# A state-space scan whose output is kept feature-major: column-tiled y products, z as a feature projection, the norm applied by a broadcast row

## The chip, the core and the metric

The kernel runs on one core of a Trainium2 chip. The metric is the device time of one execution in microseconds (us). The names used for the engines are those of the profile: PE is TensorE (matmuls), PEld its weight loads, DVE is VectorE, ACT is ScalarE, POOL is GpSimd and SP is SyncE, which here only issues transfers.

## The reference, cut to what matters

One layer of a hybrid decoder over 2048 tokens and 16 meta tokens, width 1024. A normed input `u` goes through one wide projection. Its parts feed a Mamba-2 scan (SSD, 16 heads of 64 channels in 4 groups, state 128, chunks of 128), a gated linear attention (GLA, 4 heads), and gates; two branch projections are gated, summed and projected out. The part that the change touches is the SSD branch:

```python
seg = da_cum[..., :, None] - da_cum[..., None, :]
decay = exp(where(causal, seg, -inf))
scores = einsum('bzthn,bzshn->bhzts', cc, bc)
y_diag = einsum('bhzts,bzsh,bzshp->bzthp', scores * decay, dtc, xc)
y_off  = einsum('bzthn,bzhpn,bhzt->bzthp', cc, prev, exp(da_cum))
y = y_diag + y_off + d_skip[:, None] * xs
y = y * silu(z)
y_ssd = rmsnorm(y by groups of 256 channels) * ssd_norm_w
```

## The kernel before

The tokens are done in four blocks of 512 (block 0 with the 16 meta rows besides). In a block the projections stand in this order on TensorE: four SSD groups (`ssd_proj`, L456), then four GLA heads (`gla_proj`, L654). Projections are of two kinds. `proj_feat` (L192) keeps 128 x 128 weights stationary and moves 512 tokens, so its result has features on the partitions; a tile of 128 features takes 24 matmuls, since each product of two fp32 operands is made of three fp32r products (`accum`, L186 to L190). `proj_tok` (L204) keeps 128 tokens stationary and moves 256 columns of weights, so its result has tokens on the partitions; 256 columns take 96 matmuls. Before the change z (four times) and v (four times) come from `proj_tok`, and x, B, C, q, k and the gates from `proj_feat`. For group 0 the z columns come with the 32 columns of dt and of the low-rank gate (`zm`, L462).

The scans are generators. `step()` (L813) is called behind each piece of a projection and advances every running scan by one portion, so the scans' matmuls stand in between the projections'. The order of PE and SP is as written (a manual schedule); the order of the other engines' queues is set by a scheduler when the program is built, and every engine works its queue in order.

`ssd_scan` (L502) works on one group. `before(c)` transposes x and B of chunk c to token-major (L548), makes xdt, xw and the skip term (L551 to L554), and the masked decay `dm` (Relu L560, Exp L562, mask L563) from a row `cb` of decay sums that is copied from memory to all partitions (L500, issued from ScalarE's queue, three buffers). `after(c)` makes y with `dm` stationary and xdt moving (L572), the state's part with C stationary and the state moving (L573), and the state's update (L575, L577, L578). VectorE puts y together (L580 to L585), ScalarE sums its squares (L587). At the end comes the reciprocal root (`rstd_of`, L229 to L233, with the power on GpSimd), a scaling by token (L602), eight transposes to feature-major (L607) and a scaling by feature (L609), and the result is stored.

`gla_scan` (L663) has seven steps `level(1)` to `level(64)` (L709, matmul L712), one per portion, each in a chain with a masked copy (L720), a multiply (L725) and a packing (L706), and then products by chunk (L784 to L791) and transposes (L801). PSUM has eight banks in three pools: pj with three (projections), pt with three (transposes), pc with two (scores, y and state products, `level`, the GLA products).

After the blocks come gate, branch and output stages of 512-wide matmuls, which the change does not touch.

Of the kernel before, what the change touches and what calls it, by code (L numbers as in the profile page):

```python
# [26 lines left out]
NT4 = 5  # L27
NACT = 4
NC1 = 7
# [7 lines left out]
T_GATE = 32  # L37


@with_exitstack  # L40
def trunk_kernel(ctx: ExitStack, tc: tile.TileContext, xm, xmt, w_feat, w_tok, w_zm, w_br, w_o,
# [96 lines left out]
    pv = const.tile([P, 118], F32, name="pv")  # L138
# [6 lines left out]
    d_skip = pv[:, 102:118]  # L145
# [94 lines left out]
    def load_u(b):  # L240
# [34 lines left out]
        if m0:  # L275
            rs.append(rm_s)
            nc.sync.dma_start(cst[:, :2], cf32[:, :2])
            nc.sync.dma_start(pv, pvec)
            for q in range(NWR):
                raws[f"zm_{q}"] = load_raw(w_zm[:, q * 288:(q + 1) * 288])  # L280
# [72 lines left out]
    def new_block(b, u):  # L353
        o = Block()
        o.b, o.u = b, u
        o.m0 = META if b == 0 else 0
        o.tt = o.m0 + BLK
        o.segs_all = [(0, o.tt // 2), (o.tt // 2, o.tt // 2)] if b == 0 else [(0, BLK)]
        o.segs_real = [(o.m0, BLK)]
        o.starts = [o.m0 + c * P for c in range(NCH)]  # L360
        o.chunks = ([(0, META)] if o.m0 else []) + [(a, P) for a in o.starts]
        o.ci0 = 1 if o.m0 else 0
        o.nck = len(o.chunks)
        for nm in ("tkd", "tkc", "wde", "ecu", "dec"):
            setattr(o, nm, mk(bpool, [P, 5, NH], F32, nm, bufs=2))
        o.cumd = mk(dpool, [NH, BLK], F32, "cumd")
        o.g_all = mk(bpool, [P, GH, META + BLK], F32, "g_all")
        o.gla = {}
        o.alr = mk(bpool, [P, 5, 48], F32, "alr")
        o.mov = lambda kt, a, n: tuple(t[:, kt, a:a + n] for t in u)  # L370
        return o


    def dt_chain(o, psd):
        m0, nck, ci0 = o.m0, o.nck, o.ci0
        tkd, tkc, wde, ecu, dec = o.tkd, o.tkc, o.wde, o.ecu, o.dec
# [37 lines left out]
        nc.scalar.activation(ecu[:, :nck], tkc[:, :nck], AF.Exp)  # L414
# [6 lines left out]
        nc.scalar.dma_start(o.cumd, cr)  # L421

# [32 lines left out]

    def ssd_proj(o, g):  # L456
        m0, tt = o.m0, o.tt
        feats = []
        zs = mk(wk, [P, NCH, 256], F32, "tok4", bufs=NT4)
        if g == 0:  # L460
            pss = [bank(*pl) for pl in [(pj, "pj")] * 3 + [(pt, "pt")] + ([(pc, "pc")] if m0 else [])]
            yield from proj_tok("zm", w_zm, o.u, o.starts + [0] * o.ci0, list(enumerate(pss)), 288, 1, 256)  # L462
            begin(dt_chain(o, pss[NCH:] + pss[:NCH]))
            done = [(ps[:, :256], zs[:, c]) for c, ps in enumerate(pss[:NCH])]
        else:
            pss, places = halves_of(pj, "pj")
            yield from proj_tok(f"z{g}", w_tok[g], o.u, o.starts, places)
            done = [(ps, zs[:, 2 * r:2 * r + 2].rearrange("p c f -> p (c f)")) for r, ps in enumerate(pss)]
        for ps, dst in done:
            nc.scalar.activation(dst, ps, AF.Tanh, scale=0.5)  # L470
            nc.vector.scalar_tensor_tensor(dst, dst, 1.0, ps, op0=ALU.add, op1=ALU.mult)
        yield
        for j in range(4):
# [18 lines left out]
            feats.append(f)  # L492
            yield
        begin(ssd_scan(o, g, feats, zs))
# [3 lines left out]
    def fetch_cb(o, g, c):  # L498
        cbs[g, c] = cb = mk(wk, [P, 4, P], F32, "cb", bufs=3)
        nc.scalar.dma_start(cb, o.cumd[4 * g:4 * g + 4, c * P:(c + 1) * P].unsqueeze(0).to_broadcast([P, 4, P]))  # L500

    def ssd_scan(o, g, feats, zs):  # L502
        m0, ci0 = o.m0, o.ci0
        tkd, tkc, wde, ecu, dec = o.tkd, o.tkc, o.wde, o.ecu, o.dec
        x0, x1, bf, cf = feats
        fetch_cb(o, g, 0)
        yield
# [28 lines left out]
        yt = mk(wk, [P, NCH, 256], F32, "tok4", bufs=NT4)  # L536
        ssq = mk(sm, [P, 4], F32, "ssq")
        held = {}

        def before(c):  # L540
# [6 lines left out]
            for j, f in enumerate((x0, x1, bf)):  # L547
# [6 lines left out]
            nc.vector.tensor_tensor(yt[:, c].rearrange("p (h c) -> p h c", c=64), px,  # L554
                                    hb(d_skip[:, hs], P), op=ALU.mult)
# [10 lines left out]
        def after(c):  # L566
# [4 lines left out]
            for h in range(4):  # L571
                nc.tensor.matmul(py[:, h * 64:(h + 1) * 64], dm[:, h], xdt[:, h], start=True, stop=True)  # L572
            nc.tensor.matmul(py[:, 256:512], cf[:, a:a + P], s_ssd[:, g], start=True, stop=True)  # L573
# [5 lines left out]
            yo = mk(wk, [P, 4, 64], F32, "c1", bufs=NC1)  # L579
            nc.vector.tensor_tensor(yo, py[:, 256:512].rearrange("p (h c) -> p h c", c=64),  # L580
                                    hb(ecu[:, ci, hs], P), op=ALU.mult)
            yof = yo.rearrange("p a c -> p (a c)")
            nc.vector.tensor_tensor(yof, yof, py[:, 0:256], op=ALU.add)
            nc.vector.tensor_tensor(yof, yof, yt[:, c], op=ALU.add)
            nc.vector.tensor_tensor(yt[:, c], yof, zs[:, c], op=ALU.mult)  # L585
            jk = mk(wk, [P, 256], BF16, "junk", bufs=1)
            nc.scalar.activation(jk, yt[:, c], AF.Square, accum_out=ssq[:, c:c + 1])  # L587
# [12 lines left out]
        r = rstd_of(ssq, 4, 1.0 / 1024)  # L600
        for c in range(NCH):
            nc.scalar.activation(yt[:, c], yt[:, c], AF.Identity, scale=r[:, c:c + 1])  # L602
        yield
        for j in range(2):
            ps = bank(pt, "pt")
            for c in range(NCH):
                nc.tensor.transpose(ps[:, c * P:(c + 1) * P], yt[:, c, j * P:(j + 1) * P], ident)  # L607
            yo = mk(wk, [P, BLK], F32, "gg", bufs=4)
            nc.scalar.activation(yo, ps, AF.Identity, scale=hsw[:, 2 * g + j:2 * g + j + 1])  # L609
            nc.scalar.dma_start(y_left[0][o.b][2 * g + j], yo)  # L610


    def gla_keys(o, h):
# [8 lines left out]
        o.gla[h] = [], []  # L622
# [3 lines left out]
    def gla_values(o, h):  # L626
# [9 lines left out]
        yield from proj_tok(f"v{h}", w_tok[SG + h], o.u, o.starts + [0] * o.ci0, places)  # L636
# [17 lines left out]
    def gla_proj(o, h):  # L654
        ahead = o.b == nblk - 1 and h >= GH - 2
        if not ahead or h == GH - 2:
            yield from gla_keys(o, h)
        yield from gla_values(o, h)
        if ahead and h == GH - 2:
            yield from gla_keys(o, GH - 1)  # L660
        yield from gla_out_gates(o, h)

    def gla_scan(o, h, kq, vals, gs):  # L663
# [45 lines left out]
        def level(half):  # L709
            ps = bank(pc, "pc")  # L710
# [423 lines left out]
def _layout(inputs):  # L1134
# [23 lines left out]
    feat += [cols(o_m, 2048)]  # L1158
    w_zm = tiles(np.concatenate([cols(o_z, 256), cols(o_dt, 16), cols(o_a, 16)], axis=1), 288)[0]
    w_feat = tiles(np.concatenate(feat, axis=1), P)  # L1160
    w_tok = tiles(np.concatenate([cols(o_z, 1024), cols(o_v, 1024)], axis=1), 256)
# [27 lines left out]
    d_skip = np.broadcast_to(np.asarray(inputs["d_skip"])[0][None], (P, NH))  # L1189
# [6 lines left out]
    return {"xm": xm, "xmt": xmt, "w_feat": w_feat, "w_tok": w_tok, "w_zm": w_zm, "w_br": w_br, "w_o": w_o, "cf32": cf32, "cmsk": cmsk.reshape(P, -1),  # L1196
# [21 lines left out]
```

## Time and profile before

| | |
|---|---|
| median of 3 runs | 2353.59 us (2347.39 to 2354.49) |
| the profiled execution's own time | 2356.76 us |
| its span, first to last instruction | 2355.0 us |
| mean granted TensorE clock | 0.986 |
| share of the span busy: PE, DVE, ACT, POOL | 96%, 62%, 49%, 29% |

A row of the profile that groups instructions gives the line, engine, operation, what is written and read, shape and count, then busy time, mean duration in ns, and the idle time ahead of them with what ended it. In the waits a row gives who waited for whom, the total in us, how often, and the longest. In the windows a row gives the stretch, its length, busy time and count for PE, PEld, DVE, ACT and POOL, then the granted clock, the share of the DMA engines and GB/s. In the timeline a row gives start, duration, engine, line, operation and count. Matmuls are pipelined, so that the duration of one reaches over the start of the next.

### The profile page before, as it was taken

The page shows a single profiled execution, that of the slowest core. Times are in us where ns is not written, and L with a number is a line of the kernel's source. Part 1 is how long each engine was busy: PE and PEld are TensorE (multiplying, and loading weights), DVE is VectorE, ACT ScalarE, POOL GpSimd, SP SyncE. Part 2 cuts the span into 40 slices and gives each one's busy share as a digit, 9 for nine tenths or more (in the row PEclk, how much of TensorE's full clock was granted, in tenths as well). Part 3 has the DMA queues.
Part 4 walks back from the last instruction along what each step waited for, and adds up shares of the span by engine and source line. Part 5 has one row for each costly group of instructions (what it writes and reads, how often), then busy time and mean ns, then how long its engine had stood idle before and what let it go on. Part 6 is the DMA issues. An engine that isn't in the chain of part 4 may idle for free. (4 is left out here: it accounts for less than half of the span.)

```text
span 2355.0 us, 35946 instructions
## 1 busy us (share of the span) xinstructions
PE 2261.0 (96%) x12673; PEld 1963.7 (83%) x12673; DVE 1450.1 (62%) x2547; ACT 1143.9 (49%) x2582; POOL 678.5 (29%) x681
## 2 busy tenths in 40 slices
PE   7999999999899999999999999979999999999998
PEld 6889888898788988888888888868888888888876
DVE  5666655466554466655447654455578964779776
ACT  5656544365533265633346443354545454554443
POOL 4344333122211122221112200027433355323331
PEclk9999999999999999999999999989999999999999
DMA  8666765668676676766577644457677876688743
GB/s 305 228 207 225 254 226 200 215 206 252 213 242 201 210 223 216 255 213 222 173 226 245 209 143 165 134 168 249 209 246 264 292 235 214 225 284 272 257 155 123
DMA packets 301540, 518.01 MB, mean 220 GB/s; under 512 B 27696, under 2 KB 143664, under 8 KB 301360
## 3 DMA queue, kind: packets, MB, share of 16 engines
q1 hardware_dynamic: 200400, 402.84, 52.6%
q10 hardware_dynamic: 100960, 112.88, 13.8%
q8 instruction: 99, 1.62, 0.3%
q14 instruction: 81, 0.66, 0.1%
HBM read 368.42 MB, written 147.19 MB: 219 GB/s over the span
## 5 line engine op out<-in xcount | busy, mean ns | idle before, releaser
L188 PE MATMUL pj<-u,whl 128*128 128x512 f32 (+1 forms) x1184 | 448.7, 379 | 14.4 <-ACT acc L481 7.7
L190 PE MATMUL pj<-u,whl 128*128 128x512 f32 (+1 forms) x1184 | 432.9, 366 | 1.4 <-DVE dw L391 0.8
L189 PE MATMUL pj<-u,whl 128*128 128x512 f32 (+1 forms) x1184 | 432.2, 365 | 0.0
L188 PE MATMUL pj<-whl,u 128*128 128x256 f32 (+1 forms) x992 | 291.5, 294 | 2.2 <-ACT u L306 1.5
L190 PE MATMUL pj<-whl,u 128*128 128x256 f32 (+1 forms) x992 | 283.9, 286 | 1.4 <-DVE u L308 1.4
L189 PE MATMUL pj<-whl,u 128*128 128x256 f32 (+1 forms) x992 | 283.8, 286 | 0.9 <-POOL whl L169 0.9
L188 PEld LDWEIGHTS pj<-u,whl 128*128 128x128 f32 x1184 | 226.8, 192 | 52.1 <-ACT acc L481 9.3
L188 PE MATMUL pj<-b,a 128*128 128x512 f32 x640 | 252.9, 395 | 6.0 <-ACT sn L930 3.6
L190 PEld LDWEIGHTS pj<-u,whl 128*128 128x128 f32 x1184 | 226.2, 191 | 37.6 <-POOL whl L169 1.8
L189 PEld LDWEIGHTS pj<-u,whl 128*128 128x128 f32 x1184 | 226.7, 191 | 32.2
L189 PE MATMUL pj<-b,a 128*128 128x512 f32 x640 | 250.7, 392 | 1.8 <-DVE b L889 1.8
L190 PE MATMUL pj<-b,a 128*128 128x512 f32 x640 | 251.8, 393 | 0.0
L188 PEld LDWEIGHTS pj<-whl,u 128*128 128x128 f32 x992 | 191.6, 193 | 3.8 <-ACT u L306 2.0
L190 PEld LDWEIGHTS pj<-whl,u 128*128 128x128 f32 x992 | 191.2, 193 | 2.1 <-DVE u L308 2.1
L189 PEld LDWEIGHTS pj<-whl,u 128*128 128x128 f32 x992 | 191.6, 193 | 1.5 <-POOL whl L169 1.1
L80 POOL TENSOR_TENSOR wr<-wr 128x256 f32<-128x256 f32 x80 | 65.8, 823 | 433.7 <-DMA wr<-y 146.9
L169 POOL TENSOR_TENSOR whl<-wr,whl 128x512 fp32r<-128x512 f32 (+1 forms) x100 | 132.0, 1326 | 192.8 <-ACT whl L168 167.6
L889 DVE TENSOR_TENSOR b<-br,b 128x512 fp32r<-128x512 f32 x196 | 153.8, 805 | 45.9 <-ACT b L888 41.9
L904 POOL TENSOR_TENSOR as<-ar,ar 128x512 f32<-128x512 f32 x40 | 59.2, 1481 | 403.9 <-DMA ar<-in_w_br 151.7
L485 DVE SCALAR_TENSOR_TENSOR acc<-cin,hcw,acc 128x512 f32<-128x512 f32 (+1 forms) x192 | 155.7, 811 | 31.4 <-ACT acc L481 29.8
L888 ACT ACTIVATE b<-br 128x512 fp32r<-128x512 f32 x196 | 119.5, 626 | 99.9 <-DMA br<-br_t 36.4
L914 DVE TENSOR_TENSOR a<-ar,a 128x512 fp32r<-128x512 f32 x160 | 128.6, 812 | 59.2 <-ACT a L913 58.5
(270 smaller groups left out, 4903.5 us busy)
## 6 DMA issues: line engine op xcount, KB each, us to landing
whl<-k_s SPq DMA_DIRECT2D x96, 512.0 KB, 4.6
whl<-k_g SPq DMA_DIRECT2D x96, 512.0 KB, 4.0
whl<-k_v SPq DMA_DIRECT2D x48, 512.0 KB, 3.6
whl<-k_z SPq DMA_DIRECT2D x36, 512.0 KB, 3.8
wr<-in_w_feat SPq DMA_DIRECT2D x64, 256.0 KB, 4.3
k_s<-whl SPq DMA_DIRECT2D x32, 512.0 KB, 3.7
cb<-cumd ACTq DMA_DIRECT2D x64, 256.0 KB, 6.0
y<-gg ACTq DMA_DIRECT2D x64, 256.0 KB, 5.0
```

What stands on the lines that cost most here:

```text
L80: nc.gpsimd.tensor_tensor(o, x, y, op=ALU.subtract)
L169: nc.gpsimd.tensor_tensor(hl[:, 1], raw, hl[:, 0].bitcast(F32), op=ALU.subtract)
L188: nc.tensor.matmul(ps, sh, mh, start=first, stop=False, **kw)
L189: nc.tensor.matmul(ps, sh, ml, start=False, stop=False, **kw)
L190: nc.tensor.matmul(ps, sl, mh, start=False, stop=last, **kw)
L485: nc.vector.scalar_tensor_tensor(acc, cin[:, k:k + tt], hcw[:, ti, k:k + 1], acc, op0=ALU.mult, op1=ALU.add)
L888: nc.scalar.activation(t[:, 0], raw, AF.Copy)
L889: nc.vector.tensor_tensor(t[:, 1], raw, t[:, 0].bitcast(F32), op=ALU.subtract)
L904: nc.gpsimd.tensor_tensor(s1, a21, a22, op=ALU.add)
L914: nc.vector.tensor_tensor(t[:, 1], src, t[:, 0].bitcast(F32), op=ALU.subtract)
```

## The change

z becomes a feature projection: eight tiles of 128 features in each block through `proj_feat`, two behind the x, B and C tiles of each group. The place of z's group 0 beside the dt and low-rank columns is taken by v of GLA head 0 (`first_values`), whose own projection later goes. A group's scan begins behind its last feature tile, ahead of its two z tiles. The y product now has xdt (64 columns) stationary and `dm` moving, and heads write in turn to the lower and upper 64 partitions; the state's part has the state stationary. y is kept with features on the partitions: exp of the decay sum comes as a row from memory (`ecud`) into the tile `yf`, two VectorE operations per chunk finish it, and skip, z, and squares follow once per group at full width. The sums of squares are four one-column matmuls with the squares stationary, at a stride of four columns. Their reciprocal roots are stored to memory and read back as a row on all partitions (`rb`), and one VectorE operation per tile scales by row and feature. `level` takes its bank from pt instead of pc. Buffers: tok4 5 to 6, c1 7 to 6, cb 3 to 2.

```diff
+    def first_values(o):
+        vh = mk(wk, [P, NCH, 256], F32R, "tok4", bufs=NT4)
+        vl = mk(wk, [P, NCH, 256], F32R, "tok4", bufs=NT4)
+        vm = mk(wk, [P, 256], F32, "c1", bufs=NC1)[:META] if o.m0 else None
+        pss = [bank(*pl) for pl in [(pj, "pj")] * 3 + [(pt, "pt")] + ([(pc, "pc")] if o.m0 else [])]
+        yield from proj_tok("vm", w_vm, o.u, o.starts + [0] * o.ci0, list(enumerate(pss)), 288, 1)
+        begin(dt_chain(o, pss[NCH:] + pss[:NCH]))
+        for c in range(NCH):
+            split(vh[:, c], vl[:, c], pss[c][:, :256])
...
     def ssd_proj(o, g):
...
+            if j == 3:
+                begin(ssd_scan(o, g, feats, zs))
             yield
-        begin(ssd_scan(o, g, feats, zs))
+        for j in range(2):
+            ti = 2 * g + j
+            ps, = proj_feat(f"z{ti}", w_feat[T_Z + ti], o.segs_real, o.mov)
+            zt = mk(wk, [P, BLK], F32, "gg", bufs=4)
+            nc.scalar.activation(zt, ps, AF.Tanh, scale=0.5)
+            nc.vector.scalar_tensor_tensor(zt, zt, 1.0, ps, op0=ALU.add, op1=ALU.mult)
+            zs.append(zt)
+            yield
...
-        cbs[g, c] = cb = mk(wk, [P, 4, P], F32, "cb", bufs=3)
+        cbs[g, c] = cb = mk(wk, [P, 4, P], F32, "cb", bufs=2)
...
             py = bank(pc, "pc")
             for h in range(4):
-                nc.tensor.matmul(py[:, h * 64:(h + 1) * 64], dm[:, h], xdt[:, h], start=True, stop=True)
-            nc.tensor.matmul(py[:, 256:512], cf[:, a:a + P], s_ssd[:, g], start=True, stop=True)
+                nc.tensor.matmul(py[h % 2 * 64:h % 2 * 64 + 64, h // 2 * P:(h // 2 + 1) * P], xdt[:, h], dm[:, h],
+                                 start=True, stop=True)
+            for j in range(2):
+                nc.tensor.matmul(py[:, (2 + j) * P:(3 + j) * P], s_ssd[:, g, j * P:(j + 1) * P], cf[:, a:a + P],
+                                 start=True, stop=True)
...
+            yv = yf[:, :, c * P:(c + 1) * P]
+            nc.vector.tensor_tensor(yv, py[:, 256:512].rearrange("p (j t) -> p j t", t=P), yv, op=ALU.mult)
+            nc.vector.tensor_tensor(yv, yv, py[:, :256].rearrange("p (j t) -> p j t", t=P), op=ALU.add)
...
         after(NCH - 1)
         yield
+        for j, f in enumerate((x0, x1)):
+            nc.vector.scalar_tensor_tensor(yf[:, j], f[:, m0:tt], d_skip[:, 2 * g + j:2 * g + j + 1], yf[:, j],
+                                           op0=ALU.mult, op1=ALU.add)
+            nc.vector.tensor_tensor(yf[:, j], yf[:, j], zs[j], op=ALU.mult)
+            nc.scalar.activation(zs[j], yf[:, j], AF.Square)
+        nc.vector.tensor_tensor(zs[0], zs[0], zs[1], op=ALU.add)
+        yield
+        ps = bank(pt, "pt")
         for c in range(NCH):
+            nc.tensor.matmul(ps[:, c:c + 1], zs[0][:, c::NCH], ones[:, :1], start=True, stop=True)
+        r = rstd_of(ps[:, :NCH], NCH, 1.0 / 1024)
+        nc.scalar.dma_start(o.rstd[g], r)
+        rb = mk(wk, [P, BLK], F32, "gg", bufs=4)
+        nc.scalar.dma_start(rb, o.rstd[g].rearrange("p c -> (p c)").unsqueeze(0).to_broadcast([P, BLK]))
+        yield
         yield
         for j in range(2):
+            i = 2 * g + j
+            nc.vector.scalar_tensor_tensor(yf[:, j], yf[:, j], hsw[:, i:i + 1], rb, op0=ALU.mult, op1=ALU.mult)
+            nc.scalar.dma_start(y_left[0][o.b][i], yf[:, j])
...
         def level(half):
-            ps = bank(pc, "pc")
+            ps = bank(pt, "pt")
```

In the changed kernel the y product is at L587, `level`'s matmul at L734, and the multiply by the row `rb` at L630.

More of the change, by code (lines that the diff above doesn't have):

```diff
@@ L26 @@
 NSQ = 5
-NT4 = 5
+NT4 = 6
 NACT = 4
-NC1 = 7
+NC1 = 6
 LEVELS = (1, 2, 4, 8, 16, 32, 64)
@@ L363, in new_block @@
         o.nck = len(o.chunks)
-        for nm in ("tkd", "tkc", "wde", "ecu", "dec"):
+        for nm in ("tkd", "tkc", "wde", "dec"):
             setattr(o, nm, mk(bpool, [P, 5, NH], F32, nm, bufs=2))
         o.cumd = mk(dpool, [NH, BLK], F32, "cumd")
+        o.ecud = mk(dpool, [NH, BLK], F32, "ecud")
+        o.rstd = [mk(dpool, [P, NCH], F32, f"rstd{g}") for g in range(SG)]
         o.g_all = mk(bpool, [P, GH, META + BLK], F32, "g_all")
@@ L635, in gla_values @@
             places.append((2, pv5[:, :256]))
-        yield from proj_tok(f"v{h}", w_tok[SG + h], o.u, o.starts + [0] * o.ci0, places)
+        yield from proj_tok(f"v{h}", w_tok[h], o.u, o.starts + [0] * o.ci0, places)
         if m0:
```

78 lines of the change are left out of this document (28 added, 50 removed).

## The prediction

> **What bounds the kernel now.** I read the page first (span and busy shares), then TensorE's waits, then the windows by stage, and last the timeline, where the distance between the starts of two matmuls gives what one really takes.
>
> ```profile
> span 2355.0 us, 35946 instructions
> PE 2261.0 (96%) x12673; PEld 1963.7 (83%) x12673; DVE 1450.1 (62%) x2547; ACT 1143.9 (49%) x2582; POOL 678.5 (29%) x681
> ```
>
> ```profile
> PE pc L712 <- DVE s_ssd L578: 12.3, 7, 4.0
> PE pj L188 <- ACT acc L481: 7.7, 5, 5.4
> PE pc L712 <- DVE c L583: 5.2, 5, 1.5
> PE pc L744 <- DVE c L583: 2.5, 1, 2.5
> ```
>
> ```profile
> 450.00:610.00 160.00, 160.00 (x949) 141.15 (x949) 106.65 (x207) 89.30 (x213) 40.83 (x62) 1.00 0.71 224
> 250.00:300.00 50.00, 44.52 (x274) 38.97 (x273) 32.05 (x69) 24.39 (x59) 17.27 (x15) 0.97 0.70 242
> 626.00:640.00 14.00, 8.76 (x48) 8.33 (x49) 7.21 (x16) 7.65 (x20) 5.39 (x7) 0.76 0.58 204
> 999.00:1020.00 21.00, 16.38 (x89) 14.87 (x90) 13.27 (x28) 8.46 (x23) 6.40 (x8) 0.76 0.51 176
> ```
>
> TensorE is the bound: in a whole SSD stage (450 to 610) it is busy for all 160.0 us, while VectorE has 106.65 and ScalarE 89.30. What the change is worth is therefore the TensorE time that it takes out, less the waits it puts in. The waits that exist stand where a block goes from SSD to GLA (250 to 300, 626 to 640, 999 to 1020): `level` (L712) finds both pc banks held by a chunk of the last SSD scan. After such a wait the granted clock (the column after the counts) falls to 0.76 for the window, so a wait costs more than itself.
>
> **The z and first v projections.** Busy means are no price here, since matmuls overlap; starts are.
>
> ```profile
> 723.93 0.28 PE L189 MATMUL pj<-whl,u 128*128 128x256 f32 x1
> 729.45 0.28 PE L190 MATMUL pj<-whl,u 128*128 128x256 f32 x1
> 717.26 0.40 PE L189 MATMUL pj<-u,whl 128*128 128x512 f32 x1
> 722.25 0.40 PE L190 MATMUL pj<-u,whl 128*128 128x512 f32 x1
> ```
>
> Between the first two lie 46 matmuls of one half token projection: 5.52/46 = 0.120 us each. Between the last two lie 22 of one feature tile: 4.99/22 = 0.227. The busy means (some 0.29 and 0.40 us) would promise far more. Three z projections and the separate v of head 0 go in each of four blocks, 4 x 4 x 96 matmuls, and 24 more for the meta rows: 1560, 187.2 us. Eight feature tiles of 24 come in each block: 768 x 0.227 = 174.3. Together -12.9 us. Weight loads keep their count and bytes on SP's queue.
>
> **The scan's own matmuls.**
>
> ```profile
> 642.25 1.00 PE L572 MATMUL pc<-c,sq 128*128 128x64 f32 x8
> 643.10 0.65 PE L573 MATMUL pc<-s_ssd,act 128*128 128x256 f32 x2
> 643.58 0.59 PE L575 MATMUL pc<-c,bt 128*128 128x256 f32 x2
> 645.80 0.71 PE L712 MATMUL pc<-act,c 128*128 128x128 f32 x4 [1.62 <-DVE s_ssd L578]
> 646.26 0.49 PE L188 MATMUL pj<-u,whl 128*128 128x512 f32 x1
> 722.49 1.04 PE L801 MATMUL pt<-cst,ot 128*128 128x128 f32 x8
> 723.36 0.61 PE L712 MATMUL pc<-act,c 128*128 128x128 f32 x4
> ```
>
> The state product takes 0.48 us as two instructions 256 wide; as four 128 wide at L712's pace (0.46 for four) it takes 0.46: 64 x -0.02 = -1.3 us. The eight closing transposes (0.87 us a scan) go, and four one-column fp32 products (eight instructions at L572's 0.106, which the weight load sets, 0.85) come: nothing, if the strided stationary loads as fast as a dense one.
>
> The y product stays at eight instructions, now 64 columns of weights and 128 moving. No row shows two column tiles in turn, so it has bounds. At L712's pace without overlap it is 0.92 against 0.85 us, 64 x 0.07 = +4.5. If every change of column half lets the next product run beside the last (three of eight hidden, 0.3 us), 64 x -0.3 = -20. What a change of the array's mode costs:
>
> ```profile
> 456.10 0.60 PE L418 MATMUL pt<-cst,tkc 128*16 128x128 f32 x4
> 456.46 0.48 PE L188 MATMUL pj<-u,whl 128*128 128x512 f32 x1
> 456.77 0.39 PE L189 MATMUL pj<-u,whl 128*128 128x512 f32 x1
> 138.57 0.69 PE L525 MATMUL pc<-c,bt 16*128 16x256 f32 x2
> 139.20 0.39 PE L188 MATMUL pj<-u,whl 128*128 128x264 f32 x1
> 139.43 0.28 PE L189 MATMUL pj<-u,whl 128*128 128x264 f32 x1
> ```
>
> Four transposes with 16 columns and one wide matmul take 456.10 to 456.77, 0.67 us: what four full ones and one wide matmul take (0.44 + 0.227). Narrow columns pay nothing. Two products with 16 rows take 0.63 instead of 0.48, and the matmul behind them 0.23 instead of 0.12: some 0.35 us with the entry, +22 us for 64 visits if column halves behave as rows do. The nearest row is the narrow-column one, so I take no such price, and the middle of the other bounds, -8 us. The Trainium skill (TensorEngine Tiling (Array Packing), Key Properties) says that a change of tiling mode drains the engine. The trace agrees for rows, by the 0.35 us above, and not for L418; by that rule the sum below would be 30 us worse.
>
> **The change of stage.** The scan of group 3 now begins before z, so four of its five chunk steps are done before the first `level`, and `level` takes pt's three banks instead of pc's two. The waits 12.3 + 5.2 + 2.5 = 20.0 us go, and the slow clock behind them, (1 - clock) x busy: 0.24 x 8.76 + 0.24 x 16.38 + 0.03 x 44.5 = 7.3. What is late next is one chunk and one level that still share a step: I keep 1.3 of it. -26 us.
>
> **What it adds.** VectorE and ScalarE have less work per chunk (three 256-wide VectorE operations and one Square go), which is worth nothing on the path. The norm becomes a round trip through memory.
>
> ```profile
> L231 DVE TENSOR_SCALAR rstd<-ssq x32: 157/163/171, 130.2 to 1563.3; 128x4 f32<-128x4 f32 x32
> L232 POOL TENSOR_TENSOR rstd<-rstd,mhalf x32: 999/1010/1118, 130.5 to 1563.5; 128x4 f32<-128x4 f32 x32
> DMA to landing us min/median/max: 1.6/2.7/2.9
> DMA to landing us min/median/max: 3.6/6.0/8.1
> y<-gg ACTq DMA_DIRECT2D x64, 256.0 KB, 5.0
> L560 ACT ACTIVATE sq<-cb,tkc x256: 384/387/408, 78.3 to 1375.5; 128x128 f32<-128x128 f32 x128
> 605.86 0.60 ACT L480 ACTIVATE cin<-pj 128x512 f32<-128x512 f32 x1 [1.03 <-PE pc L575]
> 611.89 0.69 DVE L491 SCALAR_TENSOR_TENSOR act<-act,acc 128x512 f32<-128x512 f32 x1 [0.17 <-ACT act L490]
> ```
>
> (The third line is the landing of L421's store of `cumd`, the nearest to a store of 2 KB; the fourth that of L500's copies of `cb`.) From the end of z's first tile: eight sums 0.85, tensor_scalar 0.16, power 1.01, store 2.7 (seven of ScalarE's Relus, 2.7 us, stand beside it), load 5.0 (`y<-gg` has its shape), issues 0.7: the row lands at 10.4. In the program as built, VectorE's queue in blocks 1 to 3 has the two multiplies by that row ahead of the mask multiply of the next scan's first chunk when group 0 hands to group 1: 2 x 0.69 + 0.69 later, at 12.5, TensorE may go on. It arrives there after sums 0.85, gates 0.45, scores 0.85, two lots of transposes 0.66 and one tile 5.45, at 8.3. A wait of 4.2 us, 2.8 to 7.3 over the 3.6 to 8.1 us that copies of `cb` take (median 6.0); I take 4.5, and 1.5 for the clock: 3 x 6 = +18 us. In the other groups the same queue has the first masks ahead of the row: no wait, as long as it lands by some 14 us. When group 3's row is awaited, the queue holds up the level chain: 1.6 us by the same count, 3 x 1.6 = +5. From the evacuation to the feature (605.86 to 612.58) pass 6.7 us, and only one tile of 5.45 and the sums 0.85 lie between now, where two halves of 5.8 lay: 0.4 short at most, 16 x 0.2 = +3. Heads 0 and 1 start closer, so one step of a block wants five pt banks and stands for two gate multiplies of 0.69: 3 x 1.5 = +4.5.
>
> `cb` has two buffers instead of three, so the copies for chunks 2 and 3 are issued shortly before their use, and ScalarE stands. One such place is in the trace already:
>
> ```profile
> 143.16 1.28 ACT L560 ACTIVATE sq<-cb,tkc 128x128 f32<-128x128 f32 x4 [2.51 <-DMA cb<-cumd]
> 144.34 0.37 ACT L480 ACTIVATE cin<-pj 128x264 f32<-128x264 f32 x1
> ```
>
> Behind the 2.51 us stood the evacuation that TensorE waited 5.4 us for (the L481 wait above). That hurts in block 0, where a feature tile takes two of three pj banks; later blocks have a tile to spare. I take +5, bounds 0 and 25. The added sum is 35.5 us.
>
> **The sum.** -12.9 - 1.3 - 8 - 26 + 35.5 = -12.7: span 2342.3. The profiled execution took 2356.76 for its 2355.0, and the median of the runs, 2353.59, is 3.2 below it: 2342.3 + 1.8 - 3.2 = 2340.9, say 2341, 0.5% faster. About 0.3% (7 us) is what a measurement of this kernel can tell from no change.
>
> **The rivals.**
> *The round trip decides* (0.30, slower). VectorE and ScalarE wait in order, so a row landing later than 14 us, not 10.4, holds up the state update or the masks in every scan. For it: `cb` copies take up to 8.1, and the power may stand behind a batch of subtractions on POOL. Against it: a tile of slack in three of four groups. 16 scans x (3.5 wait + 1.5 clock) = 80 us instead of the 26 for it above (18 + 5 + 3): 2341 + 54 = 2395, and with block 0 at its middle bound of 12, 2402; at half of that, 2371.
> *The halves run side by side and the waits are covered* (0.15): y at -20 and added waits of 10 instead of 35.5: 2341 - 12 - 25.5 = 2303. Beside it: the Trainium skill (TensorE: Matmul & The Clock Gate, Part 3: Packing small matmuls) has matmuls in different column tiles run concurrently; no run here shows it.
> *The array drains at each mode change* (0.07): y at +22 instead of -8: 2371.
> *The waits only move* (0.08): TensorE waits for pt as it did for pc, and 12 of the 26 us come back: 2353.
>
> **How the numbers follow.** My forecast has 0.40, with its own range of 2325 to 2357. Faster: 0.35 of it and the side-by-side case, 0.50 together. Same: 0.04 of it and most of the moved waits, 0.11. Slower: the round trip, the drain, the rest, 0.39. The range 2303 to 2392 reaches the side-by-side case and most of the round trip's.
>
> **What would show it.** Starts of z's matmuls 0.227 apart; L587's eight in 0.5 to 0.9 us, with no gap at either side; L734 out of TensorE's waits; a wait of L587 for VectorE's mask, once in blocks 1 to 3, ended by the landing of `gg<-rstd`. If such waits stand in most of 16 scans, or ScalarE's wait for `cb` shows in TensorE's waits beyond block 0, the forecast is wrong to the slow side; if L587's group takes near 0.55 us and no wait passes 2 us, to the fast.

## The result, and the profile after

The changed kernel takes 2376.47 us (median of 4 runs, 2372.63 to 2381.41), the kernel before 2353.77 beside it. The ratio is 1.0104 with a 95% interval of 1.0078 to 1.0130: 1.0% slower, where 0.5% faster was forecast. The profiled execution has a span of 2375.7 us and a mean granted clock of 0.979 (before: 2355.0 and 0.986).

The page of the changed kernel, the span and the engines:

```profile
span 2375.7 us, 34516 instructions
PE 2270.2 (96%) x12009; PEld 1925.5 (81%) x12009; DVE 1445.9 (61%) x2467; ACT 1091.8 (46%) x2390; POOL 679.7 (29%) x681
```

TensorE's waits after the change (waiting instruction, who ended the wait, total us, times, longest):

```profile
PE pc L808 <- DVE s_gla L809: 16.6, 10, 2.5
PE pc L551 <- DVE act L498: 11.0, 7, 2.5
PE pt L621 <- DVE gg L617: 10.7, 6, 3.5
...
PE pt L734 <- ACT c L728: 9.1, 6, 3.8
...
PE pj L189 <- ACT acc L488: 3.9, 6, 1.1
```

The waits of `level` on the pc banks (20.0 us) are gone, as forecast. New are a wait of the scores (L551) for the last feature (L498), one of the sums (L621) for the added squares (L617), and a larger one of the GLA state product (L808, 6.7 us before). `level` (L734) still waits, now for its own chain. The windows show the exchange: the two stretches that stood at 0.76 of the clock now run full, but the change of stage stands at 0.76 some 45 us later (672 to 686, a stretch that was full at 1.00 before), and the SSD stage, which had no idle time, has some.

```profile
450.00:610.00 160.00, 153.75 (x789) 125.94 (x788) 101.27 (x182) 77.84 (x179) 35.91 (x53) 0.98 0.75 225
...
626.00:640.00 14.00, 14.00 (x79) 11.28 (x78) 7.85 (x23) 6.68 (x19) 2.09 (x4) 1.00 0.98 339
672.00:686.00 14.00, 10.89 (x69) 10.50 (x68) 8.64 (x15) 3.95 (x8) 0.00 (x0) 0.76 0.71 263
999.00:1020.00 21.00, 21.00 (x119) 17.05 (x118) 11.20 (x31) 11.64 (x32) 6.64 (x9) 1.00 0.98 296
```

The terms of TensorE's own work are read from the timeline. First a y product with its neighbours, then part of a z tile, then the sums of two scans, one that waited first and one that did not:

```profile
267.88 0.39 PE L191 MATMUL pj<-u,whl 128*128 128x512 f32 x1
268.20 0.66 PE L587 MATMUL pc<-sq,c 128*64 128x128 f32 x8
268.78 0.71 PE L590 MATMUL pc<-act,s_ssd 128*128 128x128 f32 x4
269.33 0.60 PE L593 MATMUL pc<-c,bt 128*128 128x256 f32 x2
```

```profile
527.24 0.40 PE L190 MATMUL pj<-u,whl 128*128 128x512 f32 x1
...
532.04 0.39 PE L190 MATMUL pj<-u,whl 128*128 128x512 f32 x1
```

```profile
521.48 2.03 PE L621 MATMUL pt<-ones_r,gg 128*128 128x1 f32 x8 [2.42 <-DVE gg L617]
523.44 0.94 PE L448 MATMUL pj<-act,w 48*128 48x512 f32 x2
...
615.23 1.80 PE L621 MATMUL pt<-ones_r,gg 128*128 128x1 f32 x8
616.89 0.80 PE L551 MATMUL pc<-act 128*128 128x128 f32 x5
```

The y product takes 268.20 to 268.78, 0.58 us, and its entry 0.32 instead of 0.227. The same kind of place before the change:

```profile
283.08 1.00 PE L572 MATMUL pc<-c,sq 128*128 128x64 f32 x8
283.92 0.65 PE L573 MATMUL pc<-s_ssd,act 128*128 128x256 f32 x2
284.40 0.59 PE L575 MATMUL pc<-c,bt 128*128 128x256 f32 x2
```

So y went from 0.84 to 0.67 us with the entry, 64 x -0.17 = -11 us; the state product from 0.48 to 0.55, 64 x 0.07 = +4.5; z's matmuls start 4.80/21 = 0.229 apart; and the sums take 523.44 - 521.48 = 1.96 us where they waited and 616.89 - 615.23 = 1.66 where they did not, against 0.87 for the transposes that went: +0.8 to +1.1 in each of 16 scans, some +14 in all.

To see how these add up, take all distances between the starts of successive matmuls. A distance that is more than 0.45 us over the median of its kind (same line, shape and tiles) is a stall, counted with what it has over the median. What the other distances have over it in the windows in which the trace has the clock at half (11 before, 22 after) is slow clock, and the rest is work. By this count the kernel before has 2231 us of work, 80 of stalls and 23 of slow clock; the changed one 2229, 88 and 36. The work hardly fell: z and y gained what the sums and the state product lost. Stalls and clock make the loss.

### The profile page after: what moved, and what is told of

Same layout as the page of the kernel before. It is cut to its first block, busy times and chain, and to the rows that moved or that the text cites. A ratio compares the mean times of both kernels' runs of the same rounds, so it can differ in the third digit from the quotient of the medians.

```text
span 2375.7 us, 34516 instructions
## 1 busy us (share of the span) xinstructions
PE 2270.2 (96%) x12009; PEld 1925.5 (81%) x12009; DVE 1445.9 (61%) x2467; ACT 1091.8 (46%) x2390; POOL 679.7 (29%) x681
## 4 chain that ended last, share of the span: by engine, by line
PE 71%; DMA 11%; DVE 6%; issue 4%; ACT 4%; POOL 2%; SPq 1%; ACTq 1%; POOLq 0%; DVEq 0%
PE pj L189 16%; PE pj L191 16%; PE pj L190 16%; PE pt L189 3%; PE pt L191 3%; PE pt L190 3%; PE pt L734 2%; DVE acc L492 2%; PE pc L190 2%; PE pc L189 2%; PE pc L191 2%; POOL wr L81 2%; DMA gg<-rstd 2%; DMA wr<-y 1%; PE pc L590 1%
## 5 line engine op out<-in xcount | busy, mean ns | idle before, releaser
L189 PE MATMUL pj<-u,whl 128*128 128x512 f32 (+1 forms) x1440 | 554.5, 385 | 6.1 <-ACT acc L488 3.9
L191 PE MATMUL pj<-u,whl 128*128 128x512 f32 (+1 forms) x1440 | 533.4, 370 | 0.8 <-POOL whl L170 0.8
L190 PE MATMUL pj<-u,whl 128*128 128x512 f32 (+1 forms) x1440 | 533.1, 370 | 0.0
L189 PEld LDWEIGHTS pj<-u,whl 128*128 128x128 f32 x1440 | 275.9, 192 | 52.5 <-ACT acc L488 5.6
L191 PEld LDWEIGHTS pj<-u,whl 128*128 128x128 f32 x1440 | 274.3, 190 | 47.7 <-POOL whl L170 1.1
L190 PEld LDWEIGHTS pj<-u,whl 128*128 128x128 f32 x1440 | 275.7, 191 | 42.4
L189 PE MATMUL pj<-b,a 128*128 128x512 f32 x640 | 254.5, 398 | 10.1 <-ACT sn L952 8.0
L189 PEld LDWEIGHTS pj<-b,a 128*128 128x128 f32 x640 | 121.5, 190 | 38.5 <-ACT sn L952 10.2
L189 PE MATMUL pj<-whl,u 128*128 128x256 f32 (+1 forms) x480 | 143.7, 299 | 2.9 <-ACT u L307 1.5
L190 PEld LDWEIGHTS pj<-b,a 128*128 128x128 f32 x640 | 121.6, 190 | 29.0 <-DVE b L911 2.2
L191 PEld LDWEIGHTS pj<-b,a 128*128 128x128 f32 x640 | 121.5, 190 | 27.7
L191 PE MATMUL pj<-whl,u 128*128 128x256 f32 (+1 forms) x480 | 140.0, 292 | 1.4 <-DVE u L309 1.4
L190 PE MATMUL pj<-whl,u 128*128 128x256 f32 (+1 forms) x480 | 139.7, 291 | 0.0
```

The source lines that it names most:

```text
L189: nc.tensor.matmul(ps, sh, mh, start=first, stop=False, **kw)
L190: nc.tensor.matmul(ps, sh, ml, start=False, stop=False, **kw)
L191: nc.tensor.matmul(ps, sl, mh, start=False, stop=last, **kw)
```

## The experiments

Times are medians beside the kernel before on the same chip. Against the changed kernel's 2376.5, what counts is the ratio to the kernel before, 1.0104 for the changed kernel.

**The strided sums (`dense`).**

```diff
-            nc.scalar.activation(zs[j], yf[:, j], AF.Square)
+            nc.scalar.activation(zs[j].rearrange("q (c p) -> q p c", c=NCH),
+                                 yf[:, j].rearrange("q (p c) -> q p c", c=NCH), AF.Square)
...
-            nc.tensor.matmul(ps[:, c:c + 1], zs[0][:, c::NCH], ones[:, :1], start=True, stop=True)
+            nc.tensor.matmul(ps[:, c:c + 1], zs[0][:, c * P:(c + 1) * P], ones[:, :1], start=True, stop=True)
```

> The squares are written in another order of tokens, so that the one-column sums load 128 columns that lie side by side instead of every fourth; all else as in the changed kernel (2376.5 us). Strided load: the eight loads take 0.33 us each now against 0.14 to 0.19 for dense ones, and the sums 1.77 us a scan against 0.89 for the eight transposes before. Dense sums give back 16 x 0.88 = 14 us, and some of the 3 us of waits behind them: 2357 to 2363. Rival, cover: the time of the sums hides the feature's lateness, and TensorE then waits for the feature or the next row instead: 2370 to 2376, the L551 wait longer by as much as the sums are shorter.

2369.6 us, ratio 1.0055 (1.0037 to 1.0072), just below the rival's range: 7 us less by the medians, 11.5 by the ratios. The groups of the weight loads, out of the changed kernel, out of this one, and for the removed transposes out of the kernel before (busy us, mean ns):

```profile
L621 PEld LDWEIGHTS pt<-ones_r,gg 128*128 128x128 f32 x128 | 31.1, 325 | 13.6 <-DVE gg L617 13.3
```

```profile
L622 PEld LDWEIGHTS pt<-ones_r,gg 128*128 128x128 f32 x128 | 17.1, 200 | 15.8 <-DVE gg L618 15.0
```

```profile
L607 PEld LDWEIGHTS pt<-cst,tok 128*128 128x128 f32 x128 | 14.6, 141 | 0.8
```

The strided load is the cost: 325 ns against 200 with the same data side by side, 14 us less of load in 128. Part of it is not gained, as the rival says: L551's wait grows from 11.0 to 12.4 and the sums' from 10.7 to 12.5. By the count above, work falls from 2229 to 2216 us and stalls rise from 88 to 93.

**Order and halves of the y product (`order`, `onehalf`).** In the first only the loop's order changes, in the second only the place of the result. There the add reads the lower 64 partitions, and the upper half of y is left without this product.

```diff
-            for h in range(4):
+            for h in (0, 2, 1, 3):
```

```diff
-                nc.tensor.matmul(py[h % 2 * 64:h % 2 * 64 + 64, h // 2 * P:(h // 2 + 1) * P], xdt[:, h], dm[:, h],
+                nc.tensor.matmul(py[0:64, h // 2 * P:(h // 2 + 1) * P], xdt[:, h], dm[:, h],
```

> The four heads of the y product go in the order lower, lower, upper, upper half of the columns instead of lower, upper, lower, upper; all else as in the changed kernel. Side by side by halves: only at the one change of half do two products run beside each other, and a visit takes nearer 0.8 us than 0.59: 64 x 0.2 = +13, 2385 to 2390. Rival, passes: the pairs that start 7 ns apart are the two passes of one product and don't hang on the halves: no change, 2376, starts in pairs as now.

> All four heads of the y product go to the lower 64 columns of the array, and the upper half of y is left without that product; all else as in the changed kernel. Halves: the pairs of starts 7 ns apart go, the eight instructions take 0.106 each or more, a visit 0.85 us instead of 0.59, 64 x 0.26 = +17: 2393. Passes: the pairs are the two passes of one product and stay: 2376.

`order`: 2376.7 us, no change; the starts still come in pairs. `onehalf`: 2408.3 us in one run, and a visit takes 1.01 us instead of 0.58:

```profile
268.77 1.09 PE L587 MATMUL pc<-sq,c 128*64 128x128 f32 x8
269.78 0.71 PE L590 MATMUL pc<-act,s_ssd 128*128 128x128 f32 x4
```

So products in two column halves do run side by side, and it needs both halves, but not a change of half from one product to the next: my expectation for `order` was wrong in that. In `onehalf` two heads also write the same place of the bank; what that adds is not set apart.

**The round trip (`pebc`).** The row is spread by TensorE instead of by memory, with dense sums.

```diff
-        nc.scalar.dma_start(o.rstd[g], r)
-        rb = mk(wk, [P, BLK], F32, "gg", bufs=4)
-        nc.scalar.dma_start(rb, o.rstd[g].rearrange("p c -> (p c)").unsqueeze(0).to_broadcast([P, BLK]))
-        yield
+        rb = bank(pt, "pt")
+        for c in range(NCH):
+            nc.tensor.matmul(rb[:, c * P:(c + 1) * P], r[:, c:c + 1].to_broadcast([P, P]), ident, start=True, stop=True)
```

> No round trip through memory: the sums are dense, and the row of reciprocal roots is spread over the partitions by four TensorE products of a broadcast column and the identity, one portion later; the final multiply reads it from the bank. Terms only: dense sums give 14 us back and the spreading products cost 16 x 0.9 = 14: 2374 to 2379. Round trip: if VectorE's 58.5 us of waits for the row hold up TensorE through the masks and features, most of these go: 2340 to 2360.

2353.6 us, ratio 0.9989 (0.9978 to 0.9999), 23 us below `order` on the same chip, with as much TensorE work (2228 us against 2229 by the count above). The trip costs that much: 8 us of it are stalls (79 against 88) and 16 are slow clock (22 against 38). How it does is in VectorE's waits and timeline of the changed kernel:

```profile
DVE tok L630 <- DMA gg<-rstd: 58.5, 16, 6.1
```

```profile
527.40 0.41 DVE L570 TENSOR_TENSOR c<-pt,wde 128x256 f32<-128x256 f32 x1
531.49 1.42 DVE L630 SCALAR_TENSOR_TENSOR tok<-tok,hsw,gg 128x512 f32<-128x512 f32 x2 [3.67 <-DMA gg<-rstd]
532.82 1.29 DVE L578 TENSOR_TENSOR sq<-sq,sq 128x512 f32<-128x512 f32 x2
```

In all 16 scans VectorE stands for the row, 3.7 us on average, and what it has behind (here the masks) comes late. At a change of stage the level chain is behind it, and TensorE stands twice:

```profile
673.16 1.42 DVE L630 SCALAR_TENSOR_TENSOR tok<-tok,hsw,gg 128x512 f32<-128x512 f32 x2 [4.86 <-DMA gg<-rstd]
```

```profile
676.61 0.71 PE L734 MATMUL pt<-act,c 128*128 128x128 f32 x4 [1.84 <-ACT c L728]
678.59 1.22 PE L734 MATMUL pt<-act,c 128*128 128x128 f32 x4 [1.27 <-ACT c L728]
```

**The place of the row's multiplies (`dense_f`).** The trip stays; L630 is queued behind `mark["m"]`, the last mask or level multiply issued by then.

```diff
-        yield
-        yield
+        for _ in range(4):
+            yield
         for j in range(2):
             i = 2 * g + j
-            nc.vector.scalar_tensor_tensor(yf[:, j], yf[:, j], hsw[:, i:i + 1], rb, op0=ALU.mult, op1=ALU.mult)
+            with tc.issue_after(mark["m"].ins):
+                nc.vector.scalar_tensor_tensor(yf[:, j], yf[:, j], hsw[:, i:i + 1], rb, op0=ALU.mult, op1=ALU.mult)
```

> The kernel with dense sums (2369.6 us) and one change of order: the two multiplies by the row stand behind the last mask multiply of the next scan in VectorE's queue (two portions later), and behind the level chain for group 3. The round trip stays as it is. Queue order: VectorE's waits for the row (58.5 us in the changed kernel) all but go, and TensorE gets what taking the trip out got, without the 14 us of spreading products: 2336 to 2348. Rival, the trip itself (its transfers and issues on ScalarE's queue, the buffers held longer): little changes, 2362 to 2372.

2355.4 us, ratio 1.0000 (0.9981 to 1.0019), 14 us below `dense`, short of the range. VectorE's wait for the row fell as meant:

```profile
DVE tok L632 <- DMA gg<-rstd: 7.6, 2, 6.1
```

So the place in the queue was about half of what the trip cost (`pebc` gained 16 against `dense` although it adds 14 us of products). What the other half is, these runs do not settle. One thing that went with the trip and not with the place is ScalarE's wait for the copies of `cb`: 41.7 us in the changed kernel, 40.1 in `dense_f`, 20.3 in `pebc`. No run has changed that alone.

**The bank of `level` (`lvlpc`, `blvl`).** One line each way: in the changed kernel back to pc, in the kernel before to pt.

```diff
         def level(half):
-            ps = bank(pc, "pc")
+            ps = bank(pt, "pt")
```

> Only the bank of the level products goes back from the transposes' pool (three banks) to the other (two); all else as in the changed kernel (2376.5 us). Bank theory, the forecast's: the change of stage was cleared by the bank, and the waits of 20 us with 7 us of slow clock behind them come back: 2390 to 2403. Rival, earlier scan: the scan that begins two tiles sooner had cleared it already, and the bank is worth little: 2372 to 2380.

> The kernel before (2353.6 us) with one edit alone: the level products take their bank from the transposes' pool. Bank theory: the waits of L712 and L744 on the pc banks, 20 us, and most of the 7 us of slow clock behind them go: 2327 to 2338. Rival, the scan: the last scan still shares these steps, and TensorE waits at the level chain or at the transposes' banks instead: 2345 to 2356.

`lvlpc`: 2380.6 us, ratio 1.0110 (1.0089 to 1.0131), no difference from the changed kernel that can be told: the earlier scan had cleared the change of stage by itself. `blvl`: 2341.0 us, ratio 0.9936 (0.9921 to 0.9951): the bank alone, without anything else of the change, gains 0.6%. That lies between the two ranges. It is less than the waits that go, since others take their place (L786 had 6.7 us before):

```profile
PE pc L786 <- DVE s_gla L787: 11.1, 9, 2.4
PE pj L188 <- ACT acc L481: 9.5, 6, 5.4
```

**Scores and sums that wait (`late`, `pebc_sy`, `pebc_late`, `pebc_c`).** `late` and `pebc_late` put `begin(ssd_scan(...))` behind the `yield` of the last feature, as before the change; the latter without the trip. `pebc_sy` adds a `yield` ahead of the sums. `pebc_c` is `pebc_sy` with one change of order in VectorE's queue, where `mark["f"]` is the last feature's multiply (L498):

```diff
-            nc.vector.scalar_tensor_tensor(yf[:, j], f[:, m0:tt], d_skip[:, 2 * g + j:2 * g + j + 1], yf[:, j],
-                                           op0=ALU.mult, op1=ALU.add)
-            nc.vector.tensor_tensor(yf[:, j], yf[:, j], zs[j], op=ALU.mult)
+            with tc.issue_after(mark["f"].ins):
+                nc.vector.scalar_tensor_tensor(yf[:, j], f[:, m0:tt], d_skip[:, 2 * g + j:2 * g + j + 1], yf[:, j],
+                                               op0=ALU.mult, op1=ALU.add)
+                nc.vector.tensor_tensor(yf[:, j], yf[:, j], zs[j], op=ALU.mult)
```

> The scan begins one portion later, behind the step of its last feature tile, as in the kernel before; all else as in the changed kernel. Burst on VectorE and ScalarE: the closing 512-wide work of one scan then no longer meets the chain of the next group's last feature, so the waits L551 for L498 (11.0 us) and L621 for L617 (10.7) go with some seven half-clock windows at 1.5: up to -30, taken as 2350 to 2362. Rival, shift: the last group's scan runs one tile further into the level chain, and waits of L734 and L808 grow by what is gained: 2370 to 2380.

`late`: 2382.7 us, ratio 1.0124 (1.0103 to 1.0145), above both ranges and no faster than the changed kernel. L551 and the sums wait no more, but TensorE waits for z's evacuation (L507) and at the y product (L586):

```profile
PE pj L189 <- DVE gg L507: 13.5, 3, 5.1
...
PE pc L586 <- DVE tok L598: 8.8, 4, 4.3
```

> The kernel without the round trip (2353.6 us), with the sums one portion later behind the closing multiplies and squares. Lateness of the sums: L621 no longer waits for L617 (7.5 us), and three windows of half clock at 1.5 go: 2341 to 2346. Rival, the feature: the same burst on VectorE also makes the last feature late, and L551, which stands right behind the sums, waits longer by what they waited: 2350 to 2356.

> The kernel without the round trip (2353.6 us), with the scan beginning one portion later. With the row's waits gone from VectorE's queue, the later start no longer holds up z's evacuation (in the late kernel L189 waited 13.5 us for L507, and L586 8.8 for L598), and the burst theory can show: L551's 13.0 us, L621's 7.5 and some five half-clock windows at 1.5 go: 2328 to 2342. Rival, shift: what it frees comes back at z's evacuation and at the level chain as in the late kernel: 2352 to 2362.

`pebc_sy`: 2366.7 us, above both ranges and 13 slower than without the extra portion: the sums' wait went, L551's grew to 30.0 us in 13 places. `pebc_late`: 2353.1 us, no gain, as its rival had it, although L551 and the sums wait no more there either; L189 waits 11.9 us for L507.

> The kernel without the round trip and with the sums one portion later (2366.7 us, L551 waits 30.0 us for L498), and one change of order: the closing multiplies (skip and z) stand behind the next group's last feature in VectorE's queue. Burst ahead of the feature: L551's 30.0 us fall to the 9 of block 0 and the first groups, with six or more half-clock windows: 2335 to 2346. Rival, the feature's own latency: one tile of 5.45 us against 6.7 us from the evacuation to the feature leaves the wait as it is: 2358 to 2368.

`pebc_c`: 2348.7 us, ratio 0.9964 (0.9947 to 0.9980), between its two ranges and 18 us below `pebc_sy`. (The executions profiled took 2374.1 and 2338.8 us, further apart than the medians.) VectorE and then TensorE in `pebc_sy`, at the start of group 1 of block 1:

```profile
510.14 2.37 DVE L613 SCALAR_TENSOR_TENSOR tok<-act,pv,tok 128x512 f32<-128x512 f32 x2
512.44 1.22 DVE L492 SCALAR_TENSOR_TENSOR acc<-cin,hcw,acc 128x512 f32<-128x512 f32 x1
513.58 1.28 DVE L615 TENSOR_TENSOR tok<-tok,gg 128x512 f32<-128x512 f32 x2
515.74 0.69 DVE L498 SCALAR_TENSOR_TENSOR act<-act,acc 128x512 f32<-128x512 f32 x1 [0.87 <-ACT act L497]
...
520.93 0.68 DVE L498 SCALAR_TENSOR_TENSOR act<-act,acc 128x512 f32<-128x512 f32 x1
```

```profile
521.67 1.65 PE L551 MATMUL pc<-act 128*128 128x128 f32 x6 [4.26 <-DVE act L498]
```

and the same place in `pebc_c`:

```profile
511.56 2.33 DVE L492 SCALAR_TENSOR_TENSOR acc<-cin,hcw,acc 128x512 f32<-128x512 f32 x3 [0.56 <-ACT acc L488]
514.58 0.69 DVE L498 SCALAR_TENSOR_TENSOR act<-act,acc 128x512 f32<-128x512 f32 x1 [0.69 <-ACT act L497]
515.19 1.41 DVE L614 SCALAR_TENSOR_TENSOR tok<-act,pv,tok 128x512 f32<-128x512 f32 x2
```

```profile
515.33 1.16 PE L551 MATMUL pc<-act 128*128 128x128 f32 x8 [1.26 <-DVE act L498]
```

In `pebc_sy` four 512-wide closing operations (L613, L615) stand inside the third feature's chain; the fourth feature is done at 521.6, and the scores, with nothing else left ahead of them, stand for 4.26 us. With the closing work behind L498 the wait is 1.26: that is the feature's own latency, the 6.7 us against a tile of 5.45. Over the whole kernel L551's wait falls from 30.0 to 12.7 us.

**Further steps (`pl_pt`, `pl_pt_pool`, `pl_pt_pc`, `pebc_c_pt`).** In `pebc_late` and `pebc_c` the gate products L448 of blocks 1 to 3 hold two of the three pj banks while z needs one; these kernels put them into pt.

```diff
-                    ps = bank(*((pt, "pt") if i else (pj, "pj")))
+                    ps = bank(*((pt, "pt") if i or not m0 else (pj, "pj")))
```

> The kernel without the round trip and with the later scan (2353.1 us), with the gate products L448 of blocks 1 to 3 in the transposes' banks instead of the projections'. Bank of the gates: L189 no longer waits 4.0 us for L507 in three blocks, nor the L448 wait for the banks behind it, and the half clock behind goes: 2353 - 12 - 4.5, 2334 to 2342. Rival, burst: the same VectorE burst of closing multiplies is then met by the sums or by the scores one step later: 2348 to 2355.

> As the kernel with the gates in the transposes' banks, and the two multiplies by z (L615 in the changed kernel) on GpSimd. Burst: VectorE's closing work falls from 3.9 to 2.5 us a scan, and if it is what makes sums and features late, another 3 to 8 us go against that kernel. Rival, latency: 1.4 us or more per multiply on GpSimd, behind its own queue, makes the sums later than they were, and TensorE waits for them: 3 to 10 us slower than that kernel.

> As the kernel with the gates in the transposes' banks, with the level products back in the other pool. Transposes' banks crowded: with sums, rows, gates and levels in three banks, giving the levels back gains 2 to 8 us. Bank theory: the last scan now runs one tile further into the levels, so the waits on its two banks come back: 5 to 15 us slower than that kernel.

`pl_pt`: 2343.6 us, ratio 0.9945 (0.9930 to 0.9960), between its two ranges. With the z multiplies on GpSimd 2351.7 (0.9968 to 1.0003), with the levels back in pc 2354.8 (0.9984 to 1.0018): each came out as the second of its two theories had it. With the scan one tile later the bank matters again.

> The kernel at 2348.7 us (no trip, closing multiplies behind the last feature) with the gate products in the transposes' banks. The wait of L189 for L508 (5.3 us in three blocks) and some half clock behind it go: 2338 to 2344. Rival, crowded banks: sums, rows, gates and levels share three banks, and the wait moves to L448 or L551: 2347 to 2352.

`pebc_c_pt`: 2341.0 us, ratio 0.9938 (0.9920 to 0.9957). By the medians this and `blvl` are the fastest versions run, and both beat both kernels.

**All of it with the trip kept (`dense_fc`, `dl_pt_f`, `dense_fc3_pt`).** Combinations of the edits above: `dense_fc` is dense sums, a portion more ahead of them, and both changes of order; `dl_pt_f` is `pl_pt` with dense sums and the trip, L630 behind the masks; `dense_fc3_pt` is `dense_fc` with L630 behind the last feature and the gates in pt.

> Dense sums one portion later, the round trip kept, with both changes of order: closing multiplies behind the last feature, row multiplies behind the masks. If order is the whole of (1) and (2), this has the 14 us of dense sums besides: 2322 to 2336, below both kernels. If either is latency, 2345 to 2360.

> Dense sums, the round trip kept, the scan one portion later, the gate products in the transposes' banks, and the row's multiplies behind the masks: the version at 2343.6 us with the spreading products (16 x 0.89 = 14 us of TensorE) replaced by a trip that nothing waits for. Queue order: 2327 to 2336. Rival, the trip itself: 2345 to 2358.

> Dense sums one portion later, the round trip kept, the closing multiplies behind the last feature, and the row's multiplies now behind the last feature of the scan after that, four tiles behind the sums; gate products in the transposes' banks. Order theory: VectorE's waits for the row fall from 55.9 us to under 10, L587's 12 us of waits go, and 14 us less of TensorE's own work than in the kernel without the trip remain: 2330 to 2342. Rival, the burst moved: closing and row multiplies stand together behind the feature, 5.3 us of VectorE, and masks and z come late instead: 2346 to 2358.

None came into its range: 2356.9 us (0.9974 to 1.0003), 2348.0 (0.9945 to 0.9986) and 2376.6 (1.0060 to 1.0116). The first two lie in their rivals' ranges, the third above both. In `dense_fc` the sums moved but the row's multiplies did not move as far, and VectorE waited for the row again:

```profile
DVE tok L634 <- DMA gg<-rstd: 55.9, 8, 10.7
```

In `dense_fc3_pt` they stand with the closing work behind the feature, and the sums pay for it, not the masks and z that its rival named:

```profile
PE pt L624 <- DVE gg L619: 25.1, 9, 6.3
```

The order theory alone thus does not give the forecast sum; a 512-wide VectorE operation has to stand somewhere between two features, and each place tried has brought waits of its own.

## Why the prediction was wrong

**The bound.** TensorE is the bound in both kernels, and the reading that the change is worth its TensorE time less the waits it adds held. The forecast was -12.7 us of span and the trace has +20.7, a miss of 33.4. By the count of starts, 20 of it lie in TensorE's own work (-22.2 forecast, -2 measured) and 13 in stalls and clock together (+9.5 forecast, +22 measured).

**z and first v, -12.9.** Right per instruction: 0.229 between starts against the 0.227 taken. Over all projections the count of starts gives 1121 us before and 1112 after, -9.

**The scan's own matmuls, -1.3 - 8 + 0.** The state product was +4.5, not -1.3: two 128-wide pairs do not follow each other at `level`'s pace here. The y product was -11, better than the -8 taken; the halves do run side by side. The Trainium skill (TensorEngine Tiling (Array Packing), Key Properties) says that a change of tiling mode drains the engine: the trace shows an entry longer by 0.09 us, a quarter of the 0.35 by which that rival was priced, 64 x 0.09 = 6 us that are in the -11 already. The sums are **the first step that failed**: "nothing, if the strided stationary loads as fast as a dense one". It does not; 325 ns against 200, and some 14 us of TensorE's work, which `dense` takes out. The Trainium skill (Advanced Engine Details and Errata, SBUF Cachelines) says that an access which goes to another 16-byte line each time pays a penalty. With every fourth fp32 value each access does, and the trace agrees by the 325 ns; the prediction named the condition and did not weigh it.

**The change of stage, -26.** The 20.0 us of waits on the pc banks went, but neither `level` nor the slow clock left the change of stage: L734 waits 9.1 us for L728 (5.0 for L706 before), and 672 to 686 stands at 0.76. What came back there is the row's, below. And the reason given for it was half right: the earlier scan did it, and the bank added nothing that `lvlpc` could show, though alone it gains 13 us on the kernel before.

**The round trip, +18 + 5.** Its size was about right (23 us by `pebc`) and its place wrong. I let VectorE be held by the row only where group 0 hands to group 1. It is held in all 16 scans, for 58.5 us, and L587's own wait for the mask is 1.0 us in all; what stands behind L630 comes late instead, of which the level chain is shown above. The row landed 10.0 to 15.3 us after its sums began (10.4 forecast), and the limit of 14 us for "no wait" failed: two rows that landed after 10.0 us held VectorE for 3.7 and 6.1. This is the mechanism of the rival that had 0.30, and the time fell into that rival's 2371 to 2402. That the time fell there is luck: its full price was 80 us, while the trip made about 23, near the 26 that the forecast had for it, and the other terms brought the time into that range.

**Scores and feature lateness, +3. The second step that failed.** L551 and L621 wait 21.7 us, and half-clock windows follow most of these waits. The latency was counted from an undisturbed feature (6.7 us). But the closing work of a scan, which the prediction passed over as less work for VectorE, "worth nothing on the path", comes as one burst of 512-wide operations. L621's 10.7 us are waits for that work itself, all in blocks 1 to 3. With the sums a portion later, it also stands inside the next group's feature chain and holds up the scores: of the 30.0 us in `pebc_sy`, 17 and 18 us of time hang on its place, as `pebc_c` shows. For L551 in the changed kernel this is not shown: 8.3 of its 11.0 us stand in block 0, the first of them (2.5) where no scan has closed yet, and 12.7 us are left in `pebc_c`. Nor are the 21.7 us all to be had: `late` and `pebc_late` were rid of both waits and no faster.

**Banks of pt +4.5, `cb` with two buffers +5.** Neither shows on TensorE. L189's wait for L488 fell from 7.7 to 3.9, and the waits for the gates' L451 all but went. On ScalarE the wait for `cb` did come, 41.7 us in 20 places instead of 12.2 in 8:

```profile
ACT sq L575 <- DMA cb<-cumd: 41.7, 20, 4.5
```

No run gave the third buffer back, so what this is worth stays open.

**Not in the forecast.** L808's wait for the GLA state update rose from 6.7 to 16.6 us, where VectorE has a feature's or a gate's multiply ahead of L809. It was 9 to 15 in every variant, `blvl` among them; its cause was not isolated.

In TensorE's own work the terms close: the strided sums +14, the state product +6 and z +4 over their forecasts, y -3 under its own, 21 against the 20 counted. Stalls and clock do not close term by term (waits of the scores and sums +19, L808 +10, slow clock +13 in all, against them the terms for banks and `cb` that did not come on TensorE), since the slow clock follows several waits at once and some waits took the place of others.

## What to carry to other kernels

An engine that is 61% busy can still set the time through the order of its queue: ask of every wide operation that a change gathers into one place what stands behind it there, and of every wait for memory what is queued behind it, in each repetition and not only in the one where the order looks bad. Take the layout of a stationary operand as a cost until a load of that layout has been timed. Try the smallest part of a change alone: here one line, the bank of `level`, gained 0.6% and the rest of the change took more than that back.

## What the runs showed of the hardware

- A stationary operand of every fourth fp32 value loads in 325 ns, against 200 with the same values side by side.
- Two 64-column products run side by side also when their order is lower, lower, upper, upper; with all in one half a visit takes 1.01 us instead of 0.58.
- The clock can fall after short waits too, but not each time. At one place of the changed kernel TensorE waits 0.76 and then 0.90 us, with the strided sums between, and the window around it shows 0.79. The same two waits in the next block (0.77 and 0.90) left it at 1.00:

```profile
568.00:576.00 8.00, 6.33 (x27) 5.61 (x26) 5.71 (x11) 4.67 (x14) 1.01 (x1) 0.79 0.44 148
948.00:956.00 8.00, 6.33 (x33) 5.40 (x32) 6.18 (x11) 5.07 (x16) 1.01 (x1) 1.00 0.46 155
```
